# S5 output operands from one stored tile, chunk states later, scan coefficients in PSUM

## The chip, the cores and the metric

The kernel runs on one core of a Trainium2 chip. The metric is the device time of one execution in microseconds, the lower the better.

## What is computed

A decoder trunk of two layers on 256 positions of 2048 channels, in float32. Each layer is a mixer and a convolutional feed-forward network (FFN, inner width 5632), each followed by a layer norm. The even layer's mixer is gated linear attention beside block-sparse attention. The odd layer's mixer, where the change lies, is a gated DeltaNet of eight heads (GDN) beside an S5 state-space layer:

```
def s5_ssm(u, ...):   # u: 256 positions, 64 groups of 16 channels; 64 complex states per group
    bu_re = jnp.einsum('gpc,bsgc->bsgp', bb_re, u)
    bu_im = jnp.einsum('gpc,bsgc->bsgp', bb_im, u)
    ...
    _, _, x_re, x_im = lax.associative_scan(complex_affine_combine, elems, axis=1)
    return (jnp.einsum('gcp,bsgp->bsgc', c_re, x_re) - jnp.einsum('gcp,bsgp->bsgc', c_im, x_im) + d * u)

def odd_mixer(x, w_in, ...):
    qkv, z, beta_in, decay_in, u = split_cols(x @ w_in, ODD_SIZES)
    ...
    o = gated_delta_chunked(q, k, v, g, beta)
    o = rms_norm(o, norm_g) * jax.nn.silu(z.reshape(hs).astype(jnp.float32))
    y = jax.nn.gelu(s5_ssm(u, ...))
    s5_out = y * jax.nn.sigmoid(y @ glu_w + glu_b)
    return jnp.concatenate([gdn_out, s5_out], axis=-1) @ w_out
```

## The kernel before

**Weights.** Every matrix product is made of three products of split operands. A weight group of 1 MB (512 rows by 512 columns) is loaded by the sync engine's queue (SP) into `raw` (three buffers), ACT writes its rounded half `hi` (L130), DVE the rest `lo` (L131), in two halves of a group; the pools hold four groups of `hi` and `lo` ahead. PE then makes 48 matmuls for a group (L152 to L154, in `proj_a`, accumulators `acc`), so 192 for 512 columns. `proj_b` does the same with the weights moving (L185 to L188).

**The odd mixer.** `odd_mixer` projects u (the input of S5), writes it to `Ud` and reads it back as chunks of eight positions (`uim`). Then a loop `hf` over the two halves of the heads runs three projections, `kind` 0 to 2 (q, k, v), each followed by a short convolution (`eq`: ACT L847, DVE L849 on the rows of 512 columns) and a norm (`norms`: PE L809, POOL L818), and then two generators of `gdn_pair` in lockstep, the chain of small dependent steps of the gated DeltaNet (L897 to L972). Inside that chain the projection z of the half (`zp`) is called. Below, GDN0 and GDN1 are the chains of hf 0 and hf 1.

**The S5 layer.** It is woven into this by `plan`, a table that hangs hooks on the weight groups of the projections.
- Chunk states: for each of four pairs of blocks, `VTd` is loaded (L1022), PE makes the states (`prod`, L1032), and PE and DVE turn them into `X5` (`back`, L1041 and L1044). X5 takes 31 steps of two times 32 numbers per partition.
- `s5_scan` runs over X5 on DVE, 30 steps of five instructions: t1 (L1055) and the two halves of t2 (L1056, L1057) are products of the step before with the coefficients `a8`; L1058 adds t2 to t1, L1059 adds t1 to the step's own entry.
- `s5_outputs`: for each of eight blocks `operands` loads `CAd` (512 KB, L1075) and eight shifted windows of `Gd` (64 KB each, L1077, together TP) into buffers that two blocks take in turn, and POOL copies the block's states out of X5 (L1081, twice a block). `prod` multiplies `uim` with TP (L1092, does not need the scan) and the states with CA (L1097, does). ACT copies two blocks out, `back` transposes (L1106), ACT applies GELU (L1107), and after each four blocks eight stores write `Yd` (L1111).
- `s5_y` loads Yd back in two halves (L1119), ACT and DVE split it (L1123, L1124), `s5_glu` multiplies it with its weights, and then the out-projection of the mixer begins with L185.

`Gd`, `CAd` and `VTd` are made in the first FFN as background jobs: `s5_prep_small`, then `s5_prep_block(b)` for the eight blocks, one for each pair of the FFN's up-projections.

**What sets the order.** A scheduler orders each engine's instructions when the kernel is built, from the program's order and a simulation of the engines; at run time each engine takes its queue strictly in order, and SP, which issues nearly every DMA, too: an instruction that waits holds all that is queued behind it. `self.ps()` hands out four PSUM buffers in turn, which the GDN chains, the S5 steps and the norms share.

Of the kernel before, what the change touches and what calls it, by code (L numbers as in the profile page):

```python
# [7 lines left out]
F32 = mybir.dt.float32  # L8
F32R = mybir.dt.float32r
AF = mybir.ActivationFunctionType  # L10
ALU = mybir.AluOpType
# [4 lines left out]
P = 128  # L16
# [46 lines left out]
class Build:  # L63
# [511 lines left out]
    def s5_prep_small(self):  # L575
# [61 lines left out]
        self.a8 = a8  # L637
        dr = lambda nm, s: self.drp.tile(s, F32, name=nm)
        self.VTd, self.CAd = dr("VTd", [8, P, 2, 4, P]), dr("CAd", [8, P, 2, 4, P])
        self.Gd = dr("Gd", [64, 16, 256])  # L640
        self.Ud, self.Yd = dr("Ud", [1024, 256]), dr("Yd", [1024, 256])
        dT = wk.tile([P, 8], F32, name="s_d")
        nc.sync.dma_start(dT, I["s5d"])
# [2 lines left out]
        nc.gpsimd.memset(Gz, 0.0)  # L646
        nc.sync.dma_start(self.Gd[:, :, 0:128].rearrange("(b g) c t -> (g c) b t", b=8), Gz)

    def s5_prep_block(self, b):
        nc, I, wk = self.nc, self.I, self.wk  # L650
        G = nc.gpsimd
        ar, ai, zr, zi = self.s5p
        q0 = 4 * b
        bb = []
# [65 lines left out]
        gs = wk.tile([P, P], F32, name="s_gs")  # L720
        nc.scalar.copy(gs, ps[:, :P])
        nc.vector.scalar_tensor_tensor(gs[:, :16], self.m16, self.s5dT[:, b:b + 1], ps[:, :16], op0=ALU.mult, op1=ALU.add)
        nc.sync.dma_start(self.Gd[8 * b:8 * b + 8, :, 128:256].rearrange("g c t -> (g c) t"), gs)

    def odd_mixer(self):
# [72 lines left out]
        for hf in range(2):  # L798
            heads = []

            def norms(kind, dst):
                nonlocal cq, br, b2, n2
                sq = self.w4k((16, 0)[hf])
                nc.scalar.activation(sq, dst, AF.Square)
                pm = self.ps()
                for h in range(4):
                    for t in range(2):
                        u = 2 * h + t
                        nc.tensor.matmul(pm[:, u:u + 1], sq[:, h, t * P:t * P + P], self.ones[:, :1], start=u == 0,  # L809
                                         stop=True, skip_group_check=True)  # L810
                if kind == 0:
                    cq = sm.tile([P, 8], F32, name="cq")
                    V.tensor_scalar(cq, pm[:, :8], 1e-6, 128e-6, op0=ALU.add, op1=ALU.mult)
                else:
                    rk = sm.tile([P, 4, 2], F32, name="rk")
                    r2 = sm.tile([P, 4, 2], F32, name="r2")
                    V.tensor_scalar(rk.rearrange("p h t -> p (h t)"), pm[:, :8], 1e-6, None, op0=ALU.add)
                    nc.gpsimd.tensor_tensor(rk, rk, self.mhalf.unsqueeze(2).to_broadcast([P, 4, 2]), op=ALU.pow)  # L818
                    V.tensor_tensor(r2, rk, rk, op=ALU.mult)
                    bh = be[:, :, 4 * hf:4 * hf + 4].rearrange("p t h -> p h t")  # L820
                    br = sm.tile([P, 4, 2], F32, name="br")
                    b2 = sm.tile([P, 2, 4, 2], F32, name="b2")
                    n2 = sm.tile([P, 4], F32, name="n2")
                    V.tensor_tensor(br, bh, rk, op=ALU.mult)
                    V.tensor_tensor(b2[:, 1], bh, r2, op=ALU.mult)
                    split2(b2[:, 0], b2[:, 1])
                    V.tensor_tensor(n2, nbe[:, 4 * hf:4 * hf + 4], r2[:, :, 1], op=ALU.mult)

            if hf == 0:
                plan = [(), ([sprod[0]], [sprod[1], lambda: norms(0, heads[0]), sback[0]], [sprod[2], sback[1]],  # L830
                             [sprod[3], sback[2]]),
                        ([sback[3]], [lambda: norms(1, heads[1])])]
            else:
                op, o1, o2 = ([lambda f=f, k=k: f(k) for k in range(8)] for f in (oprep, oprod, oback))
                plan = [((), (), [op[0]], [op[1]]),
                        ([o1[0], op[2]], [o1[1], op[3], lambda: norms(0, heads[0])], [o1[2], op[4], o2[0]], [o1[3], op[5]]),
                        ([o1[4], op[6], o2[1]], [o1[5], op[7], lambda: norms(1, heads[1])], [o1[6], o2[2]], [o1[7]])]
            for kind in range(3):
                ct0 = kind * 8 + hf * 4
                dst = self.w4k(((14, 0, 1), (10, 11, 14))[hf][kind])  # L840

                def eq(accs, dst=dst, ct0=ct0):
                    for ct in range(4):
                        a = accs[ct // 2][:, (ct % 2) * T:(ct % 2) * T + T]
                        w = lambda k: cw[:, ct0 + ct, k:k + 1]
                        o = dst[:, ct, :]
                        nc.scalar.activation(o, a, AF.Identity, scale=w(3))  # L847
                        for s in range(1, 4):
                            V.scalar_tensor_tensor(o[:, s:], a[:, :T - s], w(3 - s), o[:, s:], op0=ALU.mult, op1=ALU.add)  # L849
                    nc.scalar.activation(dst, dst, AF.Silu)  # L850
                self.proj_a(w_in, ct0 * P, eq, hooks=plan[kind])
                heads.append(dst)
            if hf:
                oback(3)
            def ez(accs, ci=hf):
                for b in range(2):
                    nc.scalar.activation(zt(ci * 4 + b * 2, 2), accs[b].rearrange("p (k c) -> p k c", k=2), AF.Silu)
            zp = lambda hf=hf, ez=ez: self.proj_a(w_in, ZC + hf * 512, ez)
            self.lockstep(*(self.gdn_pair(C, heads, hf, hp, (br, b2, n2, cq), gs, ekd, zt, ng, zp) for hp in range(2)))
            if hf == 0:  # L860
                self.s5_scan()
# [186 lines left out]

    def s5_scan(self):
        V = self.nc.vector  # L1050
        a8, X = self.a8, self.X5
        for n in range(1, 31):
            t1 = self.sm.tile([P, 2, 32], F32, name="sc1")
            t2 = self.sm.tile([P, 2, 32], F32, name="sc2")
            V.tensor_tensor(t1, X[:, n - 1], a8[:, 0], op=ALU.mult)  # L1055
            V.tensor_tensor(t2[:, 0], X[:, n - 1, 1], a8[:, 1, 0], op=ALU.mult)  # L1056
            V.tensor_tensor(t2[:, 1], X[:, n - 1, 0], a8[:, 1, 1], op=ALU.mult)  # L1057
            V.tensor_tensor(t1, t1, t2, op=ALU.add)  # L1058
            V.tensor_tensor(X[:, n], X[:, n], t1, op=ALU.add)  # L1059

    def s5_outputs(self, uim):

# [9 lines left out]
        def operands(b):  # L1072
            if b == 0:
                nc.gpsimd.memset(xb, 0.0)
            nc.sync.dma_start(ca(b), self.CAd[b])  # L1075
            for s in range(8):
                nc.sync.dma_start(tp(b)[16 * s:16 * s + 16],  # L1077
                                  self.Gd[8 * b:8 * b + 8, :, 128 - 16 * s:256 - 16 * s].rearrange("g c t -> c g t"))
            for gk in range(2):
                o = 64 * gk  # L1080
                nc.gpsimd.tensor_copy(XBs[b % 2][o:o + 64, :, :, gk, 1:32],  # L1081
# [77 lines left out]
    def run(self, upto=4):  # L1159
# [6 lines left out]
        if upto >= 2:  # L1166
            bg = {1: self.s5_prep_small}
            for b in range(8):
                bg[b + 2] = lambda b=b: self.s5_prep_block(b)
            with self.phase("wk1"):  # L1170
                self.conv_ffn(0, False, bg)
            self.dump("f0")
# [71 lines left out]
```

## Time and profile before

| | us |
|---|---|
| median of three runs | 2437.14 |
| lowest and highest | 2434.97, 2440.56 |
| the profiled execution, its own time | 2437.24 |
| its span | 2435.5 |
| PE busy | 2392.0 |
| DVE, ACT, POOL busy | 1548.3, 1098.7, 520.4 |

The profile is of one execution on the one core. The parts that matter lie between 1322 and 1575 us: GDN0 starts at 1321.76 us, the S5 outputs run from 1444.96 to 1495.07 us, GDN1 from 1494.83 us, and the out-projection's first matmul starts at 1574.97 us. Busy times of several instructions that overlap are not added twice. A number in brackets at the end of a timeline row is the idle time of the engine before it, with what ended it.

### The profile page before, as it was taken

Reading aid. Unit: us, or ns where it says so; the run is one execution under the profiler, and the core shown is the slowest. Engines: PE = TensorE matmul, PEld = TensorE weight load, DVE = VectorE, ACT = ScalarE, POOL = GpSimd, SP = SyncE. Lnnn points to the kernel's source line nnn. Section 1 sums busy time; section 2 is a strip of 40 time slices with the busy share of each in tenths; the row PEclk is TensorE's granted clock in tenths of the full one; section 3 lists DMA queues with packets and bytes.
Section 4 is the critical chain, followed back from the end, with each engine's and each line's share of the span. In section 5 each row is a group of like instructions: output and inputs, shape, how many; then the busy total and the mean of one; then the engine's idle time right before and its main releaser. Section 6 shows DMA issues by size and latency. Waiting matters only on the chain.

```text
span 2435.5 us, 41498 instructions
## 1 busy us (share of the span) xinstructions
PE 2392.0 (98%) x17010; PEld 2203.0 (90%) x17010; DVE 1548.3 (64%) x2117; ACT 1098.7 (45%) x1425; POOL 520.4 (21%) x995
## 2 busy tenths in 40 slices
PE   8999999999999999999999998999999999999998
PEld 8998987999999999999799998888999999999996
DVE  5554567776655666666758854667666666666566
ACT  5633544454444454444354354543544444444442
POOL 0000002723577877730002213100000000000000
PEclk9999999999999999999999999999999999999999
DMA  7655554465555566665594368354655555555552
GB/s 252 202 167 177 197 184 162 165 219 186 200 187 181 175 213 228 209 219 198 162 301 153 122 183 216 126 187 161 221 190 186 181 188 191 186 178 191 191 185 92
DMA packets 270494, 457.19 MB, mean 188 GB/s; under 512 B 32592, under 2 KB 63696, under 8 KB 270304
## 3 DMA queue, kind: packets, MB, share of 16 engines
q1 hardware_dynamic: 270032, 454.41, 56.2%
q8 instruction: 134, 2.20, 0.4%
q14 instruction: 56, 0.46, 0.1%
q10 hardware_dynamic: 272, 0.13, 0.0%
HBM read 438.77 MB, written 15.73 MB: 187 GB/s over the span
## 4 chain that ended last, share of the span: by engine, by line
PE 88%; DVE 4%; DMA 2%; POOL 2%; SPq 1%; issue 1%; ACT 1%; DVEq 0%; ACTq 0%; POOLq 0%
PE acc L154 17%; PE acc L152 17%; PE acc L153 17%; PE acc L188 10%; PE acc L185 10%; PE acc L186 10%; PE ps L932 2%; DVE lo L131 2%; PE acc L222 1%; PE acc L221 1%; PE acc L220 1%; DMA raw<-in_even_w_in_dram 1%; DMA raw<-in_ffn_w_down_dram 0%; DVE W L273 0%; SPq L1111 0%
## 5 line engine op out<-in xcount | busy, mean ns | idle before, releaser
L131 DVE TENSOR_TENSOR lo<-raw,hi 128x1024 fp32r<-128x1024 f32 (+2 forms) x802 | 961.1, 1208 | 743.7 <-ACT hi L130 726.4
L130 ACT ACTIVATE hi<-raw 128x1024 fp32r<-128x1024 f32 (+2 forms) x802 | 818.9, 1031 | 1050.4 <-PE acc L153 529.2
L152 PE MATMUL acc<-XH,hi 128*128 128x256 f32 x3808 | 1074.7, 282 | 4.9 <-ACT hi L130 4.9
L153 PE MATMUL acc<-XL,hi 128*128 128x256 f32 x3808 | 1074.3, 282 | 0.0
L154 PE MATMUL acc<-XH,lo 128*128 128x256 f32 x3808 | 1073.2, 282 | 0.5 <-DVE lo L131 0.5
L152 PEld LDWEIGHTS acc<-XH,hi 128*128 128x128 f32 x3808 | 721.1, 189 | 8.8 <-ACT hi L130 5.3
L153 PEld LDWEIGHTS acc<-XL,hi 128*128 128x128 f32 x3808 | 721.0, 189 | 3.5 <-issue 2.1
L154 PEld LDWEIGHTS acc<-XH,lo 128*128 128x128 f32 x3808 | 720.5, 189 | 3.5 <-issue 2.5
L185 PE MATMUL acc<-hi,hh 128*128 128x512 f32 x640 | 252.8, 398 | 0.6 <-DVE W L324 0.5
L186 PE MATMUL acc<-lo,hh 128*128 128x512 f32 x640 | 253.1, 395 | 0.0
L188 PE MATMUL acc<-hi,hl 128*128 128x512 f32 x640 | 251.0, 395 | 0.0
L265 POOL TENSOR_TENSOR rs<-rs,cst 128x1 f32<-128x1 f32 x8 | 7.8, 980 | 949.8 <-DVE rs L264 949.8
L186 PE MATMUL acc<-lo,XH 128*128 128x512 f32 (+2 forms) x488 | 184.7, 379 | 3.3 <-DVE lo L131 3.3
L185 PE MATMUL acc<-hi,XH 128*128 128x512 f32 (+2 forms) x488 | 184.6, 379 | 2.3 <-ACT XH L1142 1.5
L188 PE MATMUL acc<-hi,XL 128*128 128x512 f32 (+2 forms) x488 | 167.5, 375 | 0.0
L185 PEld LDWEIGHTS acc<-hi,hh 128*128 128x128 f32 x640 | 120.2, 188 | 32.3 <-ACT W L322 2.7
L188 PEld LDWEIGHTS acc<-hi,hl 128*128 128x128 f32 x640 | 120.2, 188 | 29.1
L186 PEld LDWEIGHTS acc<-lo,hh 128*128 128x128 f32 x640 | 120.3, 188 | 27.8
L233 DVE TENSOR_TENSOR W<-W,acc 128x512 f32<-128x512 f32 x160 | 104.3, 680 | 21.3 <-PE acc L222 21.1
L186 PEld LDWEIGHTS acc<-lo,XH 128*128 128x128 f32 x488 | 92.3, 189 | 21.4 <-DVE lo L131 4.5
L185 PEld LDWEIGHTS acc<-hi,XH 128*128 128x128 f32 x488 | 92.1, 189 | 19.6 <-ACT XH L1142 1.7
L188 PEld LDWEIGHTS acc<-hi,XL 128*128 128x128 f32 x488 | 91.9, 188 | 18.1 <-DVE XL L1143 0.4
(338 smaller groups left out, 2007.7 us busy)
## 6 DMA issues: line engine op xcount, KB each, us to landing
raw<-in_ffn_w_up_dram SPq DMA_DIRECT2D x176, 1024.0 KB, 4.9
raw<-in_ffn_w_down_dram SPq DMA_DIRECT2D x88, 1024.0 KB, 5.2
raw<-in_even_w_in_dram SPq DMA_DIRECT2D x42, 1024.0 KB, 5.1
raw<-in_odd_w_in_dram SPq DMA_DIRECT2D x36, 1024.0 KB, 5.4
raw<-in_even_w_out_dram SPq DMA_DIRECT2D x16, 1024.0 KB, 4.9
raw<-in_odd_w_out_dram SPq DMA_DIRECT2D x16, 1024.0 KB, 5.2
CAd<-W SPq DMA_DIRECT2D x16, 256.0 KB, 4.4
VTd<-W SPq DMA_DIRECT2D x8, 512.0 KB, 6.6
```

The lines of the kernel that those rows point to most:

```text
L130: nc.scalar.activation(hi[:, k], r, AF.Copy)
L131: (lo_eng or nc.vector).tensor_tensor(lo[:, k], r, hi[:, k].bitcast(F32), op=ALU.subtract)
L152: nc.tensor.matmul(a, wh, xh, start=kt == 0 and ct % 2 == 0, stop=False, skip_group_check=True)
L153: nc.tensor.matmul(a, wh, xl, start=False, stop=False, skip_group_check=True)
L154: nc.tensor.matmul(a, wl, xh, start=False, stop=kt == nkt - 1, skip_group_check=True)
L185: nc.tensor.matmul(a, xh, wh, start=kt == 0, stop=False)
L186: nc.tensor.matmul(a, xh, wl, start=False, stop=False)
L188: nc.tensor.matmul(a, xl, wh, start=False, stop=kt == nkt - 1)
L220: nc.tensor.matmul(a, xh, wh, start=k == 0, stop=False)
L221: nc.tensor.matmul(a, xh, wl, start=False, stop=False)
L233: nc.vector.tensor_tensor(z, z, a, op=ALU.add)
L932: mms = lambda p, w, x: [nc.tensor.matmul(p[:, u * P:u * P + P], w[:, u, :], x[:, u, :], start=True, stop=True) for u in range(4)]
```

## The change

Three edits, in the odd mixer and in the jobs that prepare it. First, a new function `s5_prep_windows(b)` loads the eight windows of block b from Gd into slot 13 and stores the complete tile as `TPd[b]` (512 KB) in the first FFN: `s5_prep_block(b)` calls it for block b−1 and stores before its own Gd store, and a tenth background job does block 7. `s5_outputs` then loads TP by one DMA of 512 KB. Second, in `plan` of hf 0 the steps of the chunk states hang one to two weight groups later. Third, the scan's coefficients and both products lie in one PSUM buffer of `self.ps()`, filled by two copies, and t1 and t2 are added to the step's entry one after the other.

```diff
     def s5_prep_block(self, b):
         nc, I, wk = self.nc, self.I, self.wk
         G = nc.gpsimd
+        store = self.s5_prep_windows(b - 1) if b else None
...
+        if b:
+            store()
         nc.sync.dma_start(self.Gd[8 * b:8 * b + 8, :, 128:256].rearrange("g c t -> (g c) t"), gs)
...
+    def s5_prep_windows(self, b):
+        nc = self.nc
+        tp = self.w4(13).rearrange("p a (q c) -> p (a q) c", q=4)
+        for s in range(8):
+            nc.sync.dma_start(tp[16 * s:16 * s + 16],
+                              self.Gd[8 * b:8 * b + 8, :, 128 - 16 * s:256 - 16 * s].rearrange("g c t -> c g t"))
+        return lambda: nc.sync.dma_start(self.TPd[b], tp.rearrange("p g t -> p (g t)"))
...
             if hf == 0:
-                plan = [(), ([sprod[0]], [sprod[1], lambda: norms(0, heads[0]), sback[0]], [sprod[2], sback[1]],
-                             [sprod[3], sback[2]]),
-                        ([sback[3]], [lambda: norms(1, heads[1])])]
+                plan = [(), ([], [lambda: norms(0, heads[0])], [sprod[0]], [sprod[1], sback[0]]),
+                        ([sprod[2], sback[1]], [sprod[3], lambda: norms(1, heads[1]), sback[2]], [sback[3]])]
...
     def s5_scan(self):
         V = self.nc.vector
-        a8, X = self.a8, self.X5
+        X = self.X5
+        ps = self.ps()
+        two = lambda k: ps[:, 64 * k:64 * k + 64].rearrange("p (r q) -> p r q", r=2)
+        t1, t2, ar, ai = (two(k) for k in range(4))
+        V.tensor_copy(ar, self.a8[:, 0])
+        V.tensor_copy(ai, self.a8[:, 1])
         for n in range(1, 31):
-            t1 = self.sm.tile([P, 2, 32], F32, name="sc1")
-            t2 = self.sm.tile([P, 2, 32], F32, name="sc2")
-            V.tensor_tensor(t1, X[:, n - 1], a8[:, 0], op=ALU.mult)
-            V.tensor_tensor(t2[:, 0], X[:, n - 1, 1], a8[:, 1, 0], op=ALU.mult)
-            V.tensor_tensor(t2[:, 1], X[:, n - 1, 0], a8[:, 1, 1], op=ALU.mult)
-            V.tensor_tensor(t1, t1, t2, op=ALU.add)
+            V.tensor_tensor(t1, X[:, n - 1], ar, op=ALU.mult)
+            V.tensor_tensor(t2[:, 0], X[:, n - 1, 1], ai[:, 0], op=ALU.mult)
+            V.tensor_tensor(t2[:, 1], X[:, n - 1, 0], ai[:, 1], op=ALU.mult)
             V.tensor_tensor(X[:, n], X[:, n], t1, op=ALU.add)
+            V.tensor_tensor(X[:, n], X[:, n], t2, op=ALU.add)
...
             nc.sync.dma_start(ca(b), self.CAd[b])
-            for s in range(8):
-                nc.sync.dma_start(tp(b)[16 * s:16 * s + 16],
-                                  self.Gd[8 * b:8 * b + 8, :, 128 - 16 * s:256 - 16 * s].rearrange("g c t -> c g t"))
+            nc.sync.dma_start(tp(b), self.TPd[b].rearrange("p (g t) -> p g t", g=8))
...
+            bg[10] = lambda: self.s5_prep_windows(7)()
```

The scheduler orders the queues anew. On DVE, before, the scan starts during the projection of k in hf 0, its instructions (L1055 to L1059) between the convolutions L849 and the weight steps L131:

```order
L1055 TENSOR_TENSOR sc1_14350<-W_70,a8_4849 128x64
L1056 TENSOR_TENSOR sc2_14351<-W_70,a8_4849 128x32
L1057 TENSOR_TENSOR sc2_14351<-W_70,a8_4849 128x32
L849 SCALAR_TENSOR_TENSOR W_70<-acc_13110,gcw_12356,W_70 128x254
L1058 TENSOR_TENSOR sc1_14350<-sc1_14350,sc2_14351 128x64
L131 TENSOR_TENSOR lo_14091<-raw_14088,hi_14090 128x1024
L849 SCALAR_TENSOR_TENSOR W_70<-acc_13110,gcw_12356,W_70 128x253
L849 SCALAR_TENSOR_TENSOR W_70<-acc_13109,gcw_12356,W_70 128x255
L1059 TENSOR_TENSOR W_70<-W_70,sc1_14350 128x64
L849 SCALAR_TENSOR_TENSOR W_70<-acc_13109,gcw_12356,W_70 128x254
L1055 TENSOR_TENSOR sc1_14357<-W_70,a8_4849 128x64
```

In the changed kernel the scan's two copies stand behind GDN0's work, since the PSUM buffer comes free there; nine of its steps lie between the convolutions L859 (before L849) of the last projection of hf 1, and after the last of these the other 21 follow with nothing between them. Here is that place, with L1068 to L1072 for the five instructions of a step:

```order
L859 SCALAR_TENSOR_TENSOR W2_12426<-acc_15222,gcw_12429,W2_12426 128x255
L1071 TENSOR_TENSOR W_70<-W_70,ps_14423 128x64
L859 SCALAR_TENSOR_TENSOR W2_12426<-acc_15222,gcw_12429,W2_12426 128x254
L1072 TENSOR_TENSOR W_70<-W_70,ps_14423 128x64
L859 SCALAR_TENSOR_TENSOR W2_12426<-acc_15222,gcw_12429,W2_12426 128x253
L1068 TENSOR_TENSOR ps_14423<-W_70,ps_14423 128x64
L1069 TENSOR_TENSOR ps_14423<-W_70,ps_14423 128x32
L1070 TENSOR_TENSOR ps_14423<-W_70,ps_14423 128x32
L1071 TENSOR_TENSOR W_70<-W_70,ps_14423 128x64
L1072 TENSOR_TENSOR W_70<-W_70,ps_14423 128x64
```

What moved is the whole scan, by some 100 rows of DVE, from beside the weight steps of hf 0 to behind the last of those of hf 1. In the changed kernel each of the five instructions of a step carries a wait on DVE itself; before, L1056 and L1057 carried none.

On PE, before, the matmuls of the S5 outputs (L1092, L1097, L1106) of the eight blocks stand between weight matmuls of hf 1's projections, as here, in the middle of the k and v projections:

```order
L1092 MATMUL ps_15259<-W_70 32x128 x4
L1097 MATMUL ps_15259<-W_70 32x128 x8
L1092 MATMUL ps_15259<-W_70 32x128 x4
L1097 MATMUL ps_15259<-W_70 32x128 x8
L1106 MATMUL ps_15295<-cst_84,W_70 128x128 x4
L809 MATMUL ps_15404<-cst_84,W_70 128x1 x8
L152 MATMUL acc_15248<-XH1_81,hi_15565 128x256
L153 MATMUL acc_15248<-XL1_83,hi_15565 128x256
L154 MATMUL acc_15248<-XH1_81,lo_15566 128x256
L1092 MATMUL ps_15259<-W2_12353,W_70 32x128 x4
L1097 MATMUL ps_15259<-W_70 32x128 x8
L1092 MATMUL ps_15259<-W2_12353,W_70 32x128 x4
```

In the changed kernel (L1103, L1108, L1117 for the three) only the first four L1103 stand there. The weight matmuls of k, v and of the whole z projection of hf 1 follow each other, 366 of them, and behind the last of them the S5 outputs come in one piece, up to the first matmul of GDN1 (L907, before L897):

```order
L153 MATMUL acc_15972<-XL1_83,hi_16153 128x256
L154 MATMUL acc_15972<-XH1_81,lo_16154 128x256
L1108 MATMUL ps_14848<-W_70 32x128 x8
L1103 MATMUL ps_14848<-W_70 32x128 x4
L1108 MATMUL ps_14848<-W_70 32x128 x8
L1103 MATMUL ps_14848<-W2_12426,W_70 32x128 x4
L1108 MATMUL ps_14848<-W_70 32x128 x8
L1103 MATMUL ps_14848<-W2_12426,W_70 32x128 x4
L1108 MATMUL ps_14848<-W_70 32x128 x8
L1103 MATMUL ps_15034<-W_70 32x128 x4
L1108 MATMUL ps_15034<-W_70 32x128 x8
L1103 MATMUL ps_15034<-W_70 32x128 x4
```

What moved is all of the S5 outputs, behind 192 matmuls of z that before stood in GDN1. From the second L373 of GDN0 to GDN1's first matmul there are 381 weight matmuls now and were 191; from GDN0's first matmul to that L373 579 and 639; from GDN1's first to the out-projection's first L185 192 and 322. From the second pair of L914 and L915 of GDN1 (now L924, L925) to that L185 there are 192 and were 240.

On SP, before, the loads of a block stand as one of CAd and eight of Gd; in the changed kernel the loads of blocks 2 to 7 stand like this, behind the last weight group of z (the first row):

```order
L117 DMA raw_16147<-in_odd_w_in_dram 128x4x512
L1089 DMA W_70<-TPd_4857 128x1024
L1088 DMA W_70<-CAd_4855 128x1024
L1089 DMA W2_12426<-TPd_4857 128x1024
L1088 DMA W_70<-CAd_4855 128x1024
L1089 DMA W_70<-TPd_4857 128x1024
L1088 DMA W_70<-CAd_4855 128x1024
L1089 DMA W2_12426<-TPd_4857 128x1024
L290 DMA W_70<-Xd_79 128x2x512
L1088 DMA W_70<-CAd_4855 128x1024
L1089 DMA W_70<-TPd_4857 128x1024
L1088 DMA W_70<-CAd_4855 128x1024
```

Each such load waits until the matmuls of the block two before have freed its buffer. Behind these rows come the first eight stores of Yd, the rest of the loads, the load of Yd's first half, its other eight stores and the second half; the first weight group of the GLU stands behind that. What moved is that the last weight group of z now lies ahead of the loads of six blocks and no weight group lies between them.

## Rows read from the trace of the kernel before

**Rows 1.** Page, busy time and share of the span of one engine; the raw loads.
```profile
PE 2392.0 (98%) x17010; PEld 2203.0 (90%) x17010; DVE 1548.3 (64%) x2117; ACT 1098.7 (45%) x1425; POOL 520.4 (21%) x995
...
raw<-in_ffn_w_up_dram SPq DMA_DIRECT2D x176, 1024.0 KB, 4.9
```

**Rows 2.** Waits of PE: line waited for, releaser, us in total, times, longest.
```profile
PE ps L1092 <- DMA W<-Gd: 7.4, 4, 3.9
...
PE ps L1032 <- DMA W<-VTd: 2.3, 2, 1.7
...
PE ps L932 <- DVE W L944: 1.8, 1, 1.8
```

**Rows 3.** Windows: stretch, length, busy time of each engine, granted clock, DMA share, GB/s.
```profile
1321.76:1444.43 122.67, 117.55 (x973) 116.40 (x972) 94.13 (x203) 55.45 (x95) 31.33 (x24) 0.97 0.38 124
...
1444.43:1494.83 50.40, 43.04 (x630) 39.97 (x628) 18.03 (x33) 18.17 (x23) 10.89 (x14) 0.97 0.89 216
...
1511.47:1574.97 63.50, 59.75 (x493) 58.64 (x493) 41.60 (x47) 31.91 (x50) 13.93 (x8) 0.97 0.49 169
...
480.00:1060.00 580.00, 579.41 (x4201) 540.03 (x4200) 367.50 (x433) 260.21 (x309) 365.09 (x790) 1.00 0.58 196
...
1270.00:1280.00 10.00, 7.69 (x87) 7.02 (x86) 3.32 (x6) 6.00 (x6) 0.00 (x0) 1.00 1.00 354
```

**Rows 4.** Windows again, one stretch, instructions that touch the tile acc alone.
```profile
1297.10:1314.28 17.18, 17.18 (x144) 17.13 (x144) 5.09 (x12) 1.37 (x3) 1.00 0.48 159
```

**Rows 5.** Timeline of DVE, one uncontended scan step: start, length, line, operation.
```profile
1311.21 0.23 DVE L1055 TENSOR_TENSOR sc<-W,a 128x64 f32<-128x64 f32 x1
1311.35 0.19 DVE L1056 TENSOR_TENSOR sc<-W,a 128x32 f32<-128x32 f32 x1
1311.46 0.18 DVE L1057 TENSOR_TENSOR sc<-W,a 128x32 f32<-128x32 f32 x1
1311.68 0.22 DVE L1058 TENSOR_TENSOR sc<-sc,sc 128x64 f32<-128x64 f32 x1
1311.93 0.23 DVE L1059 TENSOR_TENSOR W<-W,sc 128x64 f32<-128x64 f32 x1
1312.19 0.23 DVE L1055 TENSOR_TENSOR sc<-W,a 128x64 f32<-128x64 f32 x1
```

**Rows 6.** Groups by line: busy time and mean ns, idle time before, releaser.
```profile
L1081 POOL COPY W<-W 64x248 f32<-64x248 f32 x16 | 12.7, 797 | 25.8 <-PE ps L1097 25.3
...
L944 DVE TENSOR_TENSOR W<-W,ps 128x512 f32<-128x512 f32 x36 | 24.5, 684 | 13.9 <-PE ps L932 13.9
...
L926 DVE TENSOR_TENSOR W<-cst,W 128x512 f32<-128x512 f32 x4 | 2.7, 678 | 0.0
...
L849 DVE SCALAR_TENSOR_TENSOR W<-acc,gcw,W 128x255 f32<-128x255 f32 (+2 forms) x72 | 32.4, 475 | 6.7 <-ACT W L847 6.3
...
L131 DVE TENSOR_TENSOR lo<-raw,hi 128x1024 fp32r<-128x1024 f32 (+2 forms) x802 | 961.1, 1208 | 743.7 <-ACT hi L130 726.4 <-PE acc L154 12.9
```

**Rows 7.** Timeline of PE in the S5 outputs, then of their last block.
```profile
1470.82 0.43 PE L1092 MATMUL ps<-W 128*32 128x128 f32 x8
...
1471.50 0.40 PE L1092 MATMUL ps<-W 128*32 128x128 f32 x8
...
1494.47 0.60 PE L1106 MATMUL ps<-cst,W 128*128 128x128 f32 x4
```

**Rows 8.** DMA issues between 1430 and 1500 us: count, KB each, median us to landing.
```profile
W<-CAd SPq DMA_DIRECT2D x8, 512.0 KB, 4.9
...
raw<-in_odd_w_in_dram SPq DMA_DIRECT2D x3, 1024.0 KB, 6.9
```

**Rows 9.** Timeline after the last block: ACT, ACT, then PE.
```profile
1508.77 1.15 ACT L1123 ACTIVATE XH<-raw 128x512 fp32r<-128x512 f32 x2 [6.33 <-DMA raw<-Yd]
...
1511.48 1.06 ACT L130 ACTIVATE hi<-raw 128x1024 fp32r<-128x1024 f32 x1 [1.56 <-DMA raw<-in_glu_w_dram]
...
1574.97 0.50 PE L185 MATMUL acc<-hi,XH 128*128 128x512 f32 x1 [1.47 <-ACT XH L1142]
```

More of the change, by code (lines that the diff above doesn't have):

```diff
@@ L639, in s5_prep_small @@
         self.VTd, self.CAd = dr("VTd", [8, P, 2, 4, P]), dr("CAd", [8, P, 2, 4, P])
-        self.Gd = dr("Gd", [64, 16, 256])
+        self.Gd, self.TPd = dr("Gd", [64, 16, 256]), dr("TPd", [8, P, 1024])
         self.Ud, self.Yd = dr("Ud", [1024, 256]), dr("Yd", [1024, 256])
```

## The prediction

> **What bounds the kernel now.** I read the page's busy times first: PE is busy 2392.0 of 2435.5 us [rows 1], so 43 us of idle time is all that any edit can remove, and what an edit can add is any wait that leaves PE without weight matmuls. Next the waits of PE: those that the edits aim at are small, 7.4 us for the Gd windows before L1092 and 2.3 us for VTd before L1032 [rows 2]. Then the windows of the odd mixer [rows 3]: GDN0 is 122.67 us with PE busy 117.55, the S5 outputs 50.40 with 43.04, the end of GDN1 and the GLU 63.50 with 59.75. [...] So the stretch is nearly full, because weight matmuls fill it: in a stretch of nothing else 144 take 17.18 us, 0.119 us each, and PE is never idle [rows 4]. What the change does is therefore read from the order: where the fillers stand now, and which chain is bare without them.
>
> **The jobs in the first FFN.** They add 64 window loads and 8 stores to SP's queue and remove nothing; PE's, DVE's, ACT's and POOL's queues there are as before. Behind each store on SP wait the Gd store and the next weight loads. If SP stands for each block as long as the longest wait for windows shown, 3.9 us [rows 2], that is 8 x 3.9 = 31 us on SP, but spread over pairs, and four weight groups lie ahead of PE, 192 x 0.119 = 22.9 us of cover for each. PE was busy 579.41 of 580.00 us there [rows 3]. Bounds 0 and 3; I take 0.
>
> **The chunk states.** VTd for the next pair is loaded after the product before it. The two products are now about one weight group apart, 48 x 0.119 = 5.7 us, against a landing that is 4.9 us for 512 KB in the crowded stretch [rows 8]. So the 2.3 us of waiting may go or stay; bounds 0 and -2.3, and I take 0. What is late next is the same load.
>
> **GDN0.** 60 weight matmuls leave it (639 to 579): -60 x 0.119 = -7.2. The scan leaves DVE, which was busy 94.13 of 122.67 us [rows 3], and so some waits of PE for DVE should go: I take half of the idle 5.1 us (2.6), bounds 0 and 5.1. Half of what the clock lost, 0.03 x 122.67 = 3.7 us, goes with those waits: 1.8. GDN0 to its second L373: 122.7 - 7.2 - 2.6 - 1.8 = 111.1 (107 to 115.5), so it ends at 1321.8 + 111.1 = 1432.9.
>
> **From there to the last filler.** PE then has 381 weight matmuls, 381 x 0.119 = 45.4, and the norms and first L1103, about 2.1: 47.5. PE runs out of weight matmuls at 1480.4; call this T. The Gd waits of 7.4 us are gone, and they are not in this number.
>
> **The scan is late, and it is bare.** Behind the last `lo` of z, DVE has 11 convolution steps and about one and a half scan steps, and then 21 steps alone. That last `lo` waits for a buffer that the matmuls four groups earlier free, at T - 192 x 0.119 = T - 23; with ACT's `hi`, 1.06 [rows 9], and its own 1.2 [rows 6] it ends at about T - 20. The 11 convolution steps and 7 scan instructions take 11 x 0.475 [rows 6] and 7 x 0.2, 6.6 at most, 5.6 as I take it since they overlap. The 21 steps: in the trace a step starts every 0.98 us; an instruction that does not depend on the one ahead starts after 0.11 to 0.14, one that does after 0.22 to 0.26 [rows 5]. In the changed scan every one waits for the one ahead: 0.25 + 0.22 + 0.22 + 0.25 + 0.26 = 1.20 us, 21 x 1.20 = 25.2 us. Operands in PSUM: L944 with one takes 684 ns, L926 without 678 [rows 6], so I add nothing. The scan ends at T - 20 + 5.6 + 25.2 = T + 11. Two POOL copies of 0.8 us [rows 6] with their hand-offs make it T + 13. PE stands for 13 us. Bounds: with the old 0.98 a step T + 8, less 3 if `lo` is earlier; with 0.3 us an instruction 6 more: 5 to 20.
>
> [...]
>
> **The S5 outputs without fillers.** On PE all blocks now stand in one piece. Half a block takes 0.68 us there (1470.82 to 1471.50) [rows 7], so eight blocks are 11 us of PE, and with the transposes 13.5. But blocks 2 to 7 need 1 MB each of TP and CA, in two buffers: a pair's loads start when the pair before has been multiplied. The most that DMA moved in 10 us is 354 GB/s [rows 3]; 1 MB of weights lands in 4.9 us [rows 1], of which 1.05 / 0.354 = 3.0 us is moving and 1.9 is fixed. A pair is 2.1 MB: 5.9 + 1.9 + 0.4 for hand-offs = 8.2 us, three pairs 24.6; blocks 0 and 1 and the last transposes add 3.7: 28.3 us. Before, the same loads lay beside the weight matmuls. Bounds: moving alone, 6 x 3.0 + 3.7 = 21.5; with landings like the weights' in that stretch, 6.9 us [rows 8], 33. I take 28.3, since the buffers make each pair wait. The stage ends at T + 13 + 28.3.
>
> **The Yd round trip.** From the last transposes, 1494.47 + 0.60 [rows 7], to the GLU's first `hi` at 1511.48 [rows 9] are 16.4 us: GELU, eight stores, the load, the split, the GLU's weights behind them. ACT waits 6.33 us for the load of Yd there [rows 9]. The GDN1 head and z filled PE meanwhile; z is now spent. ACT has less to do, 1.65 by its 1.06 and 0.6 for z: 14.75 (13.5 to 16.5). Up to GLU's first matmul the cover is gone, and the whole trip lies on the path.
>
> **From GLU to the out-projection.** 63.50 us [rows 3] held 240 weight matmuls, now 192: -5.7. Steps of GDN1 lose their filler: PE waited 1.8 us where L932 met DVE once [rows 2]; bounds 0 and 4, I take 2.4. Together 60.2 (58 to 62).
>
> **The sum.** 1480.4 + 13 + 28.3 + 14.75 + 60.2 = 1596.7 for the first L185, which was at 1574.97 [rows 9]: +21.7. What follows is the same code in the same order. The profiled execution took 2437.24, 0.1 from the median: 2437.2 + 21.7 = 2458.9, so **2459 us**. The bounds of the terms as independent errors (4 on GDN0, 8 on the scan, 7 on the stage, 2 on each of the other two) give 11.7.
>
> **Rivals.**
> *It does what it says.* Only waits go: 7.4 for Gd, 2.3 for VTd, the 5.1 of GDN0's idle time and the clock's 0.03 x 122.67 = 3.7 and 0.03 x 50.40 = 1.5 in GDN0 and the outputs: 2437.2 - 20.0 = 2417. For it: the waits are there [rows 2] and each edit has a clear target. Against it: the order has no filler beside the S5 outputs, and the scan's 21 steps stand behind the last `lo`; this would need PE to be covered where its queue shows nothing. 4%.
>
> *Not slower, because the bare stretch is short.* The emptied queues let the loads land early, and POOL and PE set the pace of the outputs: 13.5 to 15 us in place of 28.3, and the scan waits its lower bound of 5 in place of 13. 2458.9 - 14 - 8 = 2437. It decides where scan wait and outputs together stay below 24 us of my 41. For it: 354 GB/s in a stretch with little else [rows 3]. Against it: a load of 512 KB took 4.9 us [rows 8], and two buffers allow no load ahead. 8%.
>
> *Slower still, because the loads are slow.* With 6.9 us to landing [rows 8] the pairs take 10.2 each (+6), and the Yd trip, two such hops, 4 more: 2469. For it: DMA was 0.89 busy at only 216 GB/s in the outputs [rows 3]; against it: that was with windows of 64 KB, which are gone. 10%.
>
> **How the numbers follow.** 78% for the forecast, 8% not slower, 4% faster, 10% slower still. A measurement of this kernel can tell 0.2% from no change, 4.9 us, so 2432.3 to 2442.0. Below 2432: the 4%, and 1% of the second rival, 0.05. Within: 7% of it and 1% of the forecast's low end, 0.08. Above: 0.87. Range: 2458.9 -+ 11.7, held out to 2445 and 2471; left out are about 13% below and 7% above.
>
> **What the profile would show.** Right: no waits for Gd; behind the last weight matmul of z, PE waits 5 to 20 us at L1108 for POOL's copies; on DVE 21 steps in a row at about 1.2 us; then waits for TPd and CAd every pair of blocks, the outputs taking 21 to 33 us with PE busy 13; a wait of PE before the GLU of most of 15 us, ended by `hi`; parts of these at the lower clock; GDN0 shorter by about 11 us. Wrong: a scan that ends before T (its steps faster, or the PSUM buffer earlier), a wait in the FFN for weights, or loads of a block that land while the one before is multiplied.

## The result and the profile after

The changed kernel took 2462.16 us, the kernel before, run beside it, 2436.21 us; the ratio is 1.0094, with a 95% interval of 1.0073 to 1.0114. It is slower, by 23 us. (One disturbed run of 6215.56 us is in that median, and not in the ratio; the others took 2459.03, 2460.40 and 2463.93 us.) The profiled execution took 2459.03 us, with a span of 2457.2. Forecast were 2458.9 us and a range of 2445 to 2471.

The page's busy times of the changed kernel, which answer to [rows 1]:

```profile
PE 2401.2 (98%) x17010; PEld 2207.7 (90%) x17010; DVE 1539.8 (63%) x2119; ACT 1097.3 (45%) x1424; POOL 517.7 (21%) x995
```

PE idles 56 us of the span now and did 43.5 before, and it is busy 9 us longer with the same 17010 instructions. Nearly all of it is in the odd mixer. The waits of PE in the changed kernel (line waited for, releaser, us in total, times, longest), which answer to [rows 2]:

```profile
PE ps L1108 <- POOL W L1092: 11.0, 1, 11.0
PE ps L1108 <- DMA W<-CAd: 5.2, 4, 2.9
PE ps L1103 <- DMA W<-TPd: 4.6, 3, 2.0
PE ps L924 <- DVE W L919: 4.3, 1, 4.3
...
PE ps L1117 <- ACT W L1111: 3.7, 1, 3.7
...
PE ps L1042 <- DMA W<-VTd: 0.4, 1, 0.4
```

The 7.4 us of waits for the Gd windows are gone, and VTd costs 0.4 us instead of 2.3. In their place stand 11.0 us for POOL's first copies of the scan's result, 9.8 us for the loads of CA and TP, and 3.7 us for an ACT copy. The windows of the changed kernel: GDN0 cut as in [rows 3], then cuts at the two ends of the long wait, just ahead of GDN1's first matmul, behind GDN1's first steps, and at the out-projection (stretch, length, busy time and instructions of PE, PEld, DVE, ACT and POOL, granted clock, DMA share, GB/s):

```profile
1318.77:1425.06 106.29, 106.29 (x914) 105.92 (x912) 61.48 (x88) 51.71 (x90) 28.76 (x20) 1.00 0.40 136
1425.06:1472.70 47.64, 47.64 (x411) 47.08 (x409) 42.01 (x144) 14.90 (x19) 0.00 (x0) 1.00 0.20 72
1472.70:1483.75 11.05, 0.02 (x2) 0.00 (x1) 8.88 (x42) 0.00 (x0) 0.59 (x1) 0.64 0.00 0
1483.75:1522.40 38.65, 25.04 (x407) 20.45 (x408) 2.20 (x9) 10.11 (x14) 11.65 (x17) 0.68 0.82 245
1522.40:1542.80 20.40, 14.34 (x53) 11.55 (x52) 9.88 (x12) 8.78 (x12) 11.33 (x9) 0.58 0.74 217
1542.80:1597.00 54.20, 51.20 (x425) 49.66 (x424) 34.59 (x43) 25.63 (x44) 10.62 (x6) 0.99 0.50 162
```

The table reads from top to bottom. GDN0 is 106.29 us with PE busy all of it and the clock at 1.00. Then 47.64 us of weight matmuls with few others between them, without a break. Then 11.05 us in which PE stands and DVE works on the scan. Then the S5 outputs, 38.65 us with PE busy 25.04 and a granted clock of 0.68. Then the Yd round trip with GDN1's first steps, at 0.58, and behind the first GLU matmuls, which start at 1541.54, the clock is back at 0.99.

### The profile page after: what moved, and what is told of

Read it like the earlier page. It is cut to its first block, busy times and chain, and to the rows that moved or that the text cites. A ratio compares the mean times of both kernels' runs of the same rounds, so it can differ in the third digit from the quotient of the medians.

```text
span 2457.2 us, 41494 instructions
## 1 busy us (share of the span) xinstructions
PE 2401.2 (98%) x17010; PEld 2207.7 (90%) x17010; DVE 1539.8 (63%) x2119; ACT 1097.3 (45%) x1424; POOL 517.7 (21%) x995
## 4 chain that ended last, share of the span: by engine, by line
PE 90%; DVE 3%; issue 3%; DMA 2%; SPq 1%; ACT 0%; DVEq 0%; POOL 0%; ACTq 0%
PE acc L154 17%; PE acc L153 17%; PE acc L152 17%; PE acc L188 10%; PE acc L185 10%; PE acc L186 10%; PE ps L942 2%; DVE lo L131 1%; PE acc L222 1%; PE acc L220 1%; PE acc L221 1%; DMA raw<-in_even_w_in_dram 1%; DMA raw<-Yd 1%; DVE W L273 0%; DMA W<-CAd 0%
## 5 line engine op out<-in xcount | busy, mean ns | idle before, releaser
L131 DVE TENSOR_TENSOR lo<-raw,hi 128x1024 fp32r<-128x1024 f32 (+2 forms) x802 | 958.6, 1205 | 734.5 <-ACT hi L130 719.6
L185 PE MATMUL acc<-hi,hh 128*128 128x512 f32 x640 | 252.7, 397 | 1.0 <-DVE W L324 0.9
L185 PE MATMUL acc<-hi,XH 128*128 128x512 f32 (+2 forms) x488 | 184.6, 379 | 2.2 <-ACT XH L1153 1.5
L185 PEld LDWEIGHTS acc<-hi,hh 128*128 128x128 f32 x640 | 120.2, 188 | 32.2 <-ACT W L322 2.4
L186 PEld LDWEIGHTS acc<-lo,XH 128*128 128x128 f32 x488 | 92.3, 189 | 21.5 <-DVE lo L131 4.6
L185 PEld LDWEIGHTS acc<-hi,XH 128*128 128x128 f32 x488 | 92.1, 189 | 19.6 <-ACT XH L1153 1.6
```

The costliest lines, as they stand in the source:

```text
L131: (lo_eng or nc.vector).tensor_tensor(lo[:, k], r, hi[:, k].bitcast(F32), op=ALU.subtract)
L185: nc.tensor.matmul(a, xh, wh, start=kt == 0, stop=False)
L186: nc.tensor.matmul(a, xh, wl, start=False, stop=False)
```

## The experiments

The theory (A) was that one thing makes the loss: the PSUM buffer of the scan. `s5_scan` stands behind the GDN chains in the program, so it takes its turn in `self.ps()` behind theirs; the scan moves behind GDN0, and with it all S5 outputs move behind the last weight matmul of z. Rival B was that the stored tile or the later chunk states push the outputs back. Rival C was that the PSUM form of the scan is itself what costs. The ratios below are to the kernel before, run beside each, with 95% intervals.

**The PSUM scan alone.** The kernel before with the third edit only.

```diff
+        ps = self.ps()
+        two = lambda k: ps[:, 64 * k:64 * k + 64].rearrange("p (r q) -> p r q", r=2)
+        t1, t2, ar, ai = (two(k) for k in range(4))
+        V.tensor_copy(ar, self.a8[:, 0])
+        V.tensor_copy(ai, self.a8[:, 1])
...
-            V.tensor_tensor(t1, t1, t2, op=ALU.add)
...
             V.tensor_tensor(X[:, n], X[:, n], t1, op=ALU.add)
+            V.tensor_tensor(X[:, n], X[:, n], t2, op=ALU.add)
```

> The kernel before with the scan's coefficients and products in one PSUM buffer, and nothing else of the change. Theory A: the loss of 25 us comes from where the scan's PSUM buffer is handed out. The scan is called behind the GDN chains of hf 0, so its buffer comes free only when they end; the scan moves behind the last weight step of hf 1, and the S5 outputs behind the last weight matmul of z. Then this part alone loses as much, and a little more, since the eight window loads of each block (0.3 us of SP each) now lie bare as well: 2466 us (2456 to 2480), with one wait of PE of 8 to 14 us for POOL's first copies. Rival B: the stored tile or the moved chunk states push the outputs back, and the scan only follows: then 2432 to 2442 us, no such wait.

Measured: 2470.74 us, ratio 1.0128 (1.0110 to 1.0146). Its waits of PE:

```profile
PE ps L1095 <- DMA W<-Gd: 17.0, 5, 6.7
PE ps L1100 <- POOL W L1084: 11.0, 1, 11.0
```

The wait for POOL is the same 11.0 us to a tenth, and the windows of Gd, which cost 7.4 us between weight matmuls [rows 2], cost 17.0 where nothing lies beside them. Theory A holds and B falls: this edit alone loses more than the whole change, and the stored tile wins some of it back.

**The other two edits without it.** The scan of the kernel before in the changed kernel.

```diff
...
+            V.tensor_tensor(t1, t1, t2, op=ALU.add)
             V.tensor_tensor(X[:, n], X[:, n], t1, op=ALU.add)
-            V.tensor_tensor(X[:, n], X[:, n], t2, op=ALU.add)
```

(In this kernel t1, t2 and the coefficients lie in SBUF, as before.)

> The changed kernel with the scan of the kernel before (SBUF tiles, t2 added to t1). Theory A: the scan stands beside the weight steps of hf 0 again, the outputs between weight matmuls; the 7.4 us of waits for the Gd windows are gone and about 2 us for VTd, and GDN0 has its waits for DVE back: 2428 us (2423 to 2434). Rival B: the stored tile or the moved chunk states carry the loss: 2455 to 2465 us.

Measured: 2430.72 us, ratio 0.9955 (0.9938 to 0.9971). Faster, as A has it.

**All three edits, with the scan called earlier.** One statement moves.

```diff
+            if hf == 0:
+                self.s5_scan()
             self.lockstep(*(self.gdn_pair(C, heads, hf, hp, (br, b2, n2, cq), gs, ekd, zt, ng, zp) for hp in range(2)))
-            if hf == 0:
-                self.s5_scan()
```

> The changed kernel with all three parts, but the scan called one statement earlier, ahead of the GDN chains of hf 0, so that its PSUM buffer is handed out before theirs. Theory A (the time at which the buffer comes free): the scan is early again, and the kernel is near the one with the scan in SBUF: 2430 us (2424 to 2440), a little dearer since the chains share three buffers while the scan runs. Rival C (a scan with its operands in PSUM, five waits a step, is what costs): the scan's 30 steps of 1.23 us delay DVE's other work by some 8 us and more in contention, and at least half of the loss stays: 2446 us or more.

Measured: 2421.30 us, ratio 0.9926 (0.9910 to 0.9941), below the range expected by A, and once more:

> The changed kernel with the scan called ahead of the GDN chains, once more, beside the others of this call: 0.9926 of the kernel before, 2422 us (2418 to 2426), below the early SBUF scan by 0.2 to 0.4% by theory F, equal to it by rival G.

2422.11 us, ratio 0.9920 (0.9905 to 0.9935). The same instructions, called one statement earlier, turn a loss of 23 us into a gain of 18 to 20. So it is where the buffer is handed out that costs, and rival C falls. (A PSUM buffer outside the ring, with the call left where it was, would test the same thing alone; it was not run.) This version beats both kernels.

**The stored tile alone.** The kernel before with the first edit only.

```diff
...
-            for s in range(8):
-                nc.sync.dma_start(tp(b)[16 * s:16 * s + 16],
-                                  self.Gd[8 * b:8 * b + 8, :, 128 - 16 * s:256 - 16 * s].rearrange("g c t -> c g t"))
+            nc.sync.dma_start(tp(b), self.TPd[b].rearrange("p (g t) -> p g t", g=8))
...
```

> The kernel before with the stored operand tile alone: eight windows loaded and stored per block in the first FFN, one load of 512 KB in the outputs. Theory A: the waits for the windows (7.4 us of PE) go and part of them comes back as waits for the 512 KB loads: 2431 us (2427 to 2437). Rival B: the stores and loads in the FFN hold SP, weights come late there, and nothing is won: 2437 us or more.

Measured: 2428.09 us, ratio 0.9956 (0.9940 to 0.9972). The gain is some 11 us by the ratio, with 7 to 15 as its interval, so of the size of the removed waits, 7.4 us [rows 2]; waits for the stored tile came to 0.3 us. The FFN hides the making of the tile: PE was busy 578.40 us of the 580 us that [rows 3] cuts there, against 579.41 before.

**The later chunk states alone.** The kernel before with the second edit only, the hooks of hf 0.

```diff
-                plan = [(), ([sprod[0]], [sprod[1], lambda: norms(0, heads[0]), sback[0]], [sprod[2], sback[1]],
...
+                plan = [(), ([], [lambda: norms(0, heads[0])], [sprod[0]], [sprod[1], sback[0]]),
...
```

> The kernel before with the chunk states one to two weight groups later and nothing else. Theory A: the 2.3 us of waiting for VTd become 0.4 as in the changed kernel, the scan starts later by some weight steps and is still early enough: 2436 us (2432 to 2440), no difference that can be told. Rival: the later scan runs further into GDN0, where POOL works, and delays DVE's steps there: 2441 us or more.

Measured: 2434.75 us, ratio 0.9978 (0.9966 to 0.9990). The ratio makes a gain of some 5 us, where I had taken none. PE's waits for VTd were 0.5 us instead of 2.3, which is 1.8 of it; where the rest comes from is not shown. Beside the other edits it can't be told: the stored tile is at 0.9956 without the later states and at 0.9955 with them, and the interval of the early PSUM scan with the old hooks overlaps those of the one with the new:

> The changed kernel with the scan called ahead of the GDN chains and the chunk states where they were before. Theory A: the stored tile and the early PSUM scan carry the gain: 2422 us (2418 to 2428), as with the later states, with about 2 us of waits for VTd. Rival: the states' place decides whether the scan finishes before the outputs' copies: 2430 us or more.

Measured: 2425.47 us, ratio 0.9939 (0.9922 to 0.9955). (The edit is the one above, reversed, in the kernel with the earlier call.)

**The late scan with three waits a step.** The changed kernel, with t2 in a tile of its own in SBUF.

```diff
-        t1, t2, ar, ai = (two(k) for k in range(4))
+        t1, ar, ai = (two(k) for k in range(3))
...
         for n in range(1, 31):
+            t2 = self.sm.tile([P, 2, 32], F32, name="sc2")
```

> The changed kernel with t2 in an SBUF tile of its own, the coefficients and t1 still in PSUM; the scan stays as late, but three of its five instructions wait for the one ahead instead of five. Theory A (an instruction that waits for the one ahead on DVE starts 0.11 to 0.13 us later than one that does not): a step falls from 1.23 to about 0.98 us, the 21 bare steps by 5 us, the wait of PE for POOL's first copies from 11.0 to about 6 us, and the kernel from 2461 to 2456 us (2453 to 2459). [...]

Measured: 2450.96 us, ratio 1.0041 (1.0026 to 1.0056), against 1.0083 to 1.0094 of the changed kernel. One step of the changed kernel's bare scan and one of this kernel's, from the timeline of DVE (start, length, line, operation); first the changed kernel:

```profile
1474.39 0.23 DVE L1068 TENSOR_TENSOR ps<-W,ps 128x64 f32<-128x64 f32 x1
1474.65 0.20 DVE L1069 TENSOR_TENSOR ps<-W,ps 128x32 f32<-128x32 f32 x1
1474.88 0.20 DVE L1070 TENSOR_TENSOR ps<-W,ps 128x32 f32<-128x32 f32 x1
1475.11 0.22 DVE L1071 TENSOR_TENSOR W<-W,ps 128x64 f32<-128x64 f32 x1
1475.36 0.22 DVE L1072 TENSOR_TENSOR W<-W,ps 128x64 f32<-128x64 f32 x1
1475.62 0.23 DVE L1068 TENSOR_TENSOR ps<-W,ps 128x64 f32<-128x64 f32 x1
```

then this one, L1069 to L1073 for the five instructions:

```profile
1473.91 0.23 DVE L1069 TENSOR_TENSOR ps<-W,ps 128x64 f32<-128x64 f32 x1
1474.18 0.19 DVE L1070 TENSOR_TENSOR sc<-W,ps 128x32 f32<-128x32 f32 x1
1474.28 0.18 DVE L1071 TENSOR_TENSOR sc<-W,ps 128x32 f32<-128x32 f32 x1
1474.38 0.21 DVE L1072 TENSOR_TENSOR W<-W,ps 128x64 f32<-128x64 f32 x1
1474.63 0.22 DVE L1073 TENSOR_TENSOR W<-W,sc 128x64 f32<-128x64 f32 x1
1474.88 0.23 DVE L1069 TENSOR_TENSOR ps<-W,ps 128x64 f32<-128x64 f32 x1
```

Five waits make 1.23 us, three 0.97: L1071 and L1072 of this kernel carry no wait and start 0.10 us behind the one ahead, and where there is a wait the distance is 0.23 to 0.27. That goes with the wait and not with where t2 lies: L1070 writes SBUF, waits, and starts 0.27 us behind; L1072 reads PSUM, does not wait, and starts 0.10 us behind. Theory A's step is confirmed; with waits that cost nothing it would have stayed at 1.23 us. The effect was larger than the 5 us expected, since three more steps found room between the convolutions and 18 were left bare instead of 21: the wait for POOL's copies fell from 11.0 to 2.8 us:

```profile
PE ps L1109 <- POOL W L1093: 2.8, 1, 2.8
```

**The rounding of Yd on DVE.** The changed kernel with L1134 taken from ACT's queue.

```diff
-                nc.scalar.activation(hi, s, AF.Copy)
+                nc.vector.tensor_copy(hi, s)
```

> The changed kernel with the rounding of Yd (L1134) on DVE instead of ACT. In the changed kernel ACT waited 7.7 us for the load of Yd's first half with the copy of the last two blocks (L1111) queued behind, and PE 3.75 us for that copy. Theory E: this queue is part of the outputs' 39 us; without it the wait of 3.75 us goes and the kernel is at 2457 us (2454 to 2460). Rival: the last load of CAd (5.9 us to landing) ends the stage anyway, and nothing is gained: 2461 us.

Measured: 2460.56 us, ratio 1.0080 (1.0065 to 1.0095); the changed kernel once more, beside other runs of the kernel before:

> The changed kernel beside the others of this call: 1.0094 of the kernel before, 2461 us (2456 to 2466).

2462.58 us, ratio 1.0083 (1.0068 to 1.0097). No difference can be told, but theory E does not fall by that: the 4 us that it expected are 0.16%, about the half width of each interval. The queue was real. In the changed kernel ACT waited for Yd and then made the copy L1111 for which PE stood:

```profile
1520.13 1.15 ACT L1134 ACTIVATE XH<-raw 128x512 fp32r<-128x512 f32 x2 [7.70 <-DMA raw<-Yd]
1521.18 0.57 ACT L1111 COPY W<-ps 128x512 f32<-128x512 f32 x1
```

Without it, PE's wait for that copy is 0.75 us instead of 3.75, and the last load of CA ends the stage, as the timeline of PE in this kernel shows.

```profile
1519.27 1.08 PE L1108 MATMUL ps<-W 128*32 128x128 f32 x16 [2.64 <-DMA W<-CAd]
...
1522.38 0.90 PE L1117 MATMUL ps<-cst,W 128*128 128x128 f32 x3 [0.75 <-ACT W L1111]
```

Counted from the first matmul behind the long wait, this CA load came 1.0 us later than in the changed kernel, and the whole stage took 36.8 us against 38.8 there and 42.3 in the second profile of the changed kernel. So the rival's last load is there, but that nothing is gained is not shown: whether the queue costs up to 2 us stays open.

**The early scan in SBUF.** The two other edits, with the scan of the kernel before, called earlier. It asks why the early PSUM scan (0.992) beats the scan in SBUF (0.9955).

> The stored tile and the later chunk states, with the scan of the kernel before (SBUF), called ahead of the GDN chains as the early PSUM scan was; the two differ in where the scan's operands lie and in what the scheduler makes of that. Theory F: with both operands in SBUF a scan instruction takes up to 1 us while POOL runs, in PSUM 0.2 us; that is what the early PSUM scan gained over the scan in SBUF. Then this kernel is at 0.9955 of the kernel before, 2429 us by the first runs (2425 to 2433), and its scan takes longer on DVE than the PSUM one. Rival G: the earlier call is what gained; then it is at 0.993, 2422 us or less.

Measured, beside the early PSUM scan's 0.9920: 2429.22 us, ratio 0.9948 (0.9934 to 0.9961). The early call alone gains nothing that can be told, so rival G falls; the PSUM form, called early, gains 0.3% on it. The first instruction of a step, grouped by line, with 30 instructions, busy time and mean ns of one, in SBUF:

```profile
L1065 DVE TENSOR_TENSOR sc<-W,a 128x64 f32<-128x64 f32 x30 | 9.4, 313 | 0.6
```

and in PSUM:

```profile
L1068 DVE TENSOR_TENSOR ps<-W,ps 128x64 f32<-128x64 f32 x30 | 6.8, 226 | 0.8
```

Summed over the five lines the scan is 42.4 us of DVE in SBUF and 31.4 in PSUM. PE's waits for DVE between 1310 and 1500 us fall from 5.7 us (for W of L919, L954 and L936) to 0.8. That is 4.9 of the 7 us. The rest lies in waits for loads, 5.7 us for TP against 2.1 for TP and 1.7 for CA, and the orders of the two kernels differ there, so that part isn't shown to come from the operands.

## Why the prediction was right, and where its terms were off

The forecast held, 2458.9 for 2459.03 us of the profiled execution, and so did the mechanism in the main: the order has no filler beside the S5 outputs, the bare scan makes PE stand, and the outputs and the Yd trip follow bare. The first out-projection matmul was expected at 1596.7 us and came at 1596.80:

```profile
1596.80 0.50 PE L185 MATMUL acc<-hi,XH 128*128 128x512 f32 x1 [1.46 <-ACT XH L1153]
```

But the sum was that good because errors cancelled, and that is luck: the profiled execution was also the fastest of this kernel, and in its second profile, 2464.56 us, the S5 outputs alone took 42.3 us instead of 38.8. Step by step:

- **The first FFN**, taken at 0: PE was busy 579.01 us of the same 580 us as in [rows 3], 0.4 less. Right.
- **The chunk states**, taken at 0 with -2.3 as the other end: it was -1.9. GDN0 began 3.0 us earlier; the other 1.1 us is less than the spread of this start among the kernels run, which was between 1317 and 1324 us.
- **GDN0**, 111.1 us: it was 106.29, below the range of 107. The step that failed took half of the idle time and half of the clock's loss, and all of both went: PE is busy all of the stretch and the clock is 1.00. 122.7 - 7.2 - 5.1 - 3.7 is 106.7. The idle time goes with the scan in SBUF beside GDN0: it is 0.00 with the PSUM scan alone, too, 0.6 us with the early PSUM scan, and 4.6 to 5.8 us in the four kernels that kept the scan in SBUF. For the clock this is not shown: it was 1.00 in GDN0 also with the other two edits and with the later states alone, where the scan stayed and PE idled 4.6 and 5.2 us.
- **The fillers**, 47.5 us: 47.64. 381 matmuls at 0.119 us was the safest of the terms.
- **The scan**, 13 us of standing: 11.05. The last `lo` ended at 1452.4, which is T - 20.3 with T at 1472.7, as worked out. A step was 1.23 us where 1.20 was expected, and the 21 steps took from 1457.13 to 1482.98. The hand-off was dearer in the sum than on the chip: PE started 0.8 us after the scan's end, when the first of POOL's copies was done (0.6 us of it), and did not wait for the second.
- **The S5 outputs**, 28.3 us with bounds of 21.5 and 33: it was 38.8, to GDN1's first matmul at 1522.57. This is the term that was mis-sized. The sum had the loads set the pace, 8.2 us a pair, and 13.5 us of PE's work lie beside them. (Its upper bound should have been 34.3 by the 10.2 us a pair that the third rival has; 38.8 lies beyond either.) In the trace PE is busy 25.04 us and waits 13.5: 5.2 for CA, 4.6 for TP and 3.7 for the copy. In four parts:

```profile
1483.75:1489.30 5.55, 5.53 (x88) 4.33 (x88) 0.00 (x0) 0.00 (x0) 3.04 (x5) 0.50 0.43 124
1489.30:1499.60 10.30, 5.33 (x146) 4.02 (x146) 0.00 (x0) 3.05 (x4) 3.57 (x6) 1.00 0.91 322
1499.60:1510.40 10.80, 10.80 (x136) 9.41 (x126) 0.91 (x7) 3.43 (x5) 5.03 (x6) 0.53 0.89 222
1510.40:1522.40 12.00, 3.38 (x51) 2.69 (x52) 1.29 (x2) 3.62 (x6) 0.00 (x0) 0.62 0.87 257
```

In the first and the third part PE alone sets the pace, with the clock at 0.50 and 0.53 and no wait for a load; in the second, at 1.00, the loads do, as the sum had it. The loads of block 6 landed while block 5 was multiplied, which the prediction had named as a sign of being wrong. From one pair's first load to the next pair's it was 6.7 and 7.0 us, less than the 8.2 of the sum. So the pace of the loads was not what the term lacked. It lacked the lower clock, the norms of L820, which it had not counted in this stretch, and the last block, which had 8.6 us of waits. The clock was 0.50 in the first part, where PE was busy 5.53 of 5.55 us, 1.00 in the second, where it was busy 5.33 of 10.30, and 0.53 in the third, where it was busy all of 10.80. The norms show its price: the same 16 matmuls in the changed kernel, first behind weight matmuls, at a clock of 1.00, then in the outputs, at 0.50:

```profile
1427.81 1.84 PE L820 MATMUL ps<-cst,W 128*128 128x1 f32 x16
```

```profile
1501.06 3.41 PE L820 MATMUL ps<-cst,W 128*128 128x1 f32 x16
...
1515.70 1.08 PE L1108 MATMUL ps<-W 128*32 128x128 f32 x16 [2.90 <-DMA W<-CAd]
...
1521.80 1.11 PE L1117 MATMUL ps<-cst,W 128*128 128x128 f32 x4 [3.75 <-ACT W L1111]
1522.57 0.77 PE L907 MATMUL ps<-d_a,cr 128*128 128x512 f32 x1
```

3.41 us for 1.84. (In the second profile these norms took 1.84 us and the outputs still 42.3, with 9.8 us of waits for CA: where the low clock falls differs from one execution to the next, and no run tells the clock's part of the stage from the loads'.) The other rows are the last wait for CA and the wait for the copy. On SP the eight stores of Yd held the last loads back as SP's order would have told, had I followed it there: they took 6.29 us, and the last CA load went out at 1509.84, behind them, though the matmuls of the block two before had ended by 1507.2; that is 2.6 us at most.

```profile
1501.92 6.29 SPq L1122 DMA_DIRECT2D Yd<-W  x8
1508.32 0.95 SPq L1089 DMA_DIRECT2D W<-TPd  x1
...
1509.84 0.41 SPq L1088 DMA_DIRECT2D W<-CAd  x1
```

- **The Yd trip**, 14.75 us: from the last transposes' end at 1522.91 to the GLU's first `hi` at 1537.54, 14.6. The size is right, and no weight matmul lies beside it, as forecast. But the forecast wait of PE of most of 15 us, ended by `hi`, did not come: PE was busy 9.16 us of it with GDN1's first steps, at a clock of 0.62, and its longest wait, 4.29 us, ended with DVE's L919, right behind the split of Yd on DVE.
- **From there to the out-projection**, 60.2 us: 59.3.

So -7.7 us up to T, -2 in the scan, +10.5 in the outputs, and -1 behind them. Against the rivals: a gain from the removed waits is what the first two edits make without the third, 0.9955; the order excluded it here. That the bare stretch would be short fell with the outputs' 38.8 us. That loads would be slower was half true: CA's landed after a median of 5.6 us in that stretch, against 4.9 [rows 8], but the two pairs ahead of the last took 6.7 and 7.0 us, not 10.2.

The prediction's reading of [rows 5] and [rows 6] for DVE held. The kernel with three waits shows, for instructions of 32 and 64 columns, 0.10 us from one start to the next without a wait and 0.25 to 0.27 with one. Operands in PSUM, for which the prediction added nothing, cost 4 and 11 ns: the first instruction of a scan step, of 64 columns, took a median of 228 ns with an operand in PSUM (early PSUM scan) and of 224 with both in SBUF (early SBUF scan), the second, of 32, 195 and 184.

## What to carry to other kernels

A buffer from a shared ring is handed out in program order: a step that is put into such a ring inherits the place of its call, and moves behind what stands ahead of it in the ring. Where a change takes fillers away from a chain, go through it block by block, ask for each whether the load or PE is later, and count PE's work behind a long wait at a lower clock: here 0.50 was granted in the 5.55 us behind the wait of 11.05, and 0.68 over the whole stage. Where the idle time of a stretch is waits for one engine and that engine's load leaves, all of the idle time may go, as it did here, and not half.

## What the runs showed of the hardware

Beside POOL's work, in the rows below, the scan's instructions on DVE with both operands in SBUF took up to six times their median, 1.08 us against 0.183 (L1057), and those with one operand in PSUM 0.18 to 0.22 us. In the kernel before, a step of the scan on DVE:

```profile
1322.54 1.00 DVE L1055 TENSOR_TENSOR sc<-W,a 128x64 f32<-128x64 f32 x1
1323.46 1.05 DVE L1056 TENSOR_TENSOR sc<-W,a 128x32 f32<-128x32 f32 x1
1324.43 1.08 DVE L1057 TENSOR_TENSOR sc<-W,a 128x32 f32<-128x32 f32 x1
1325.44 0.47 DVE L849 SCALAR_TENSOR_TENSOR W<-acc,gcw,W 128x254 f32<-128x254 f32 x1
1325.83 0.97 DVE L1058 TENSOR_TENSOR sc<-sc,sc 128x64 f32<-128x64 f32 x1
```

and POOL at the same time:

```profile
1322.42 1.04 POOL L901 TENSOR_TENSOR d_a<-cst,b 128x512 fp32r<-128x512 f32 x1 [1.85 <-PE ps L898]
1323.42 2.06 POOL L896 TENSOR_TENSOR d_a<-cph,gs 128x512 fp32r<-128x512 f32 x2
1325.43 1.30 POOL L906 TENSOR_TENSOR W<-W,cph 128x512 f32<-128x512 f32 x1
```

In the kernel with the early PSUM scan, DVE, with POOL at work from 1320.95 to past 1330 us:

```profile
1321.21 0.22 DVE L1068 TENSOR_TENSOR ps<-W,ps 128x64 f32<-128x64 f32 x1
...
1323.38 0.18 DVE L1069 TENSOR_TENSOR ps<-W,ps 128x32 f32<-128x32 f32 x1
...
1325.19 0.18 DVE L1070 TENSOR_TENSOR ps<-W,ps 128x32 f32<-128x32 f32 x1
...
1326.07 0.20 DVE L1071 TENSOR_TENSOR W<-W,ps 128x64 f32<-128x64 f32 x1
```

0.97 to 1.08 us in the one, 0.18 to 0.22 in the other; over all 30 steps the longest L1055 before was 1.316 us and the longest of its counterpart 0.230. The weight steps `lo`, with two operands in SBUF, stretch in both kernels, to 2.08 us at 1326.73 before and 2.16 at 1330.80 in the other, where the median over the kernel before is 1.225. The first three of the four slow instructions, 1.00, 1.05 and 1.08 us, took about as long as the POOL instruction beside each, 1.04 us and half of 2.06; the fourth, 0.97, lay beside one of 1.30. Why they stretch is not shown.

The clock: after 11.05 us in which PE stood, the granted clock was 0.68 over the next 38.65 us (0.50, 1.00, 0.53 and 0.62 in the four parts above), 0.58 over the 20.40 us behind them, and 0.99 over the next 54.20, where weight matmuls follow each other again.
